# Moving modulation groups to VectorE and reordering the first norm of a fused two-block diffusion transformer

## The chip, the cores and the metric

One core of one Trainium2 chip runs the whole program in one launch. The metric is the device time of one execution in microseconds, as the median of several runs. Next to it stands one profiled execution, whose trace is read here.

## The reference, cut to what matters

Two small transformers run one after the other on 256 tokens `x` and 256 context tokens `ctx`, width 1024, in fp32. The first has two layers (latent attention and a Hyena convolution, then a feed-forward network), the second a gated-delta-rule layer and a gated-linear-attention (GLA) layer, each with its feed-forward network. Each layer takes six modulation vectors of 1024 from a conditioning vector:

```
mod_x = split(silu(c)     @ ada_w + ada_b, 6)     # 1024 x 6144, for x
mod_c = split(silu(c_ctx) @ ada_w + ada_b, 6)     # the same weights, for ctx
h  = rms_norm(x, g) * (1 + mod_x[1]) + mod_x[0]   # ahead of the mixer
x  = x + mod_x[2] * mixer(h)
h  = rms_norm(x, g2) * (1 + mod_x[4]) + mod_x[3]  # ahead of the network
x  = x + mod_x[5] * network(h)
```

The context stream needs chunks 0 and 1 in every layer and chunks 2 to 5 only where its output is used later, which is in the first layer of each transformer.

## The kernel before

**Layout.** Activations lie with features on the 128 partitions: `xs` is [128, 8, 512], x in columns 0 to 255 and ctx in 256 to 511. Every product is made of three fp32r products: a weight tile is split into a high part (`wh`, a cast on ScalarE, L315) and a low part (`wl`, a subtraction on VectorE, L316), activations likewise (L302, L303), and `mm3` (L324 to L326) adds high x high, high x low and low x high. One projection onto 128 features is 24 matmuls. Weights come as 512 KB transfers from SyncE's queue into three buffers.

**Modulation.** There are four matrices of 1024 x 6144: `mods[0]`, `mods[1]` for the first transformer, `mods2[0]`, `mods2[1]` for the second. `modulation` (L375) makes a list of steps, each a load and a computation. In the TensorE form (`steps`, L381) a chunk of 1024 outputs takes eight k tiles, four matmuls of 256 columns each (L402), side by side in strips of 32 columns with both conditioning vectors as the stationary operand; then a copy on ScalarE (L407), two small matmuls (L413) that bring the result into columns, and the bias (L414). In the row form (`rstep`, L434) a group of 128 outputs lies on the partitions with its 1024 weights in a row; one VectorE instruction (L437) multiplies by the conditioning vector `self.cb`, which was spread over the partitions and put through Silu (L588 to L591), and sums along the row. It serves one vector. Before, `mods[1]` and `mods2[1]` use rows for chunks 2 to 5 (32 groups, three in a step) and TensorE for chunks 0 and 1; `mods[0]` and `mods2[0]` use TensorE throughout.

**Where the steps run.** `run` (L1776) puts the steps into a queue, `self.bg`. `background(n)` takes n of them, and `load_ahead` keeps up to two loads (four at the start) ahead of the computation, in buffers of three 512 KB tiles. `quota` says how many steps a stage may take. In a feed-forward network `slot()` is called after each projection and takes a step every `every` slots. There are 56 slots in a network over both streams. Before, the first layer takes the 16 + 12 steps of `mods[0]`, its network the 17 of `mods[1]` and 18 of `mods2[0]` every 1.5 slots, and the deltanet layer's network the 17 of `mods2[1]` every 3.

**The order of the instructions.** The framework's planner orders each engine's instructions: among those that it takes to be ready by its own estimates, the one that is written first comes first. So an instruction that is ready can come ahead of work that is written before it but is not ready. `tc.issue_after` forbids that for a block on one engine. The order is fixed when the program is built; on the chip each engine works through its own.

**The norm.** `stat` adds up squares, `stat_end` takes the mean over features by a matmul with ones (L472) and the root by eleven small VectorE instructions (L457 to L464), `bcast` (L484) spreads the root over the partitions, `norm_one` (L517) makes x * r (L529, or with the factor L527), applies the factor and shift on ScalarE (L537, L540, L541) and makes high and low parts (L538, L542). In layer 0 the factors `gs` (L447, L448) come from chunk 1 of `mods[0]`, whose 16 small steps are the first thing that the program loads.

**Ends of stages.** `first_layer` computes `ys = [self.stat_end(...)]` (L1095) and then, in the return behind it, the same again for layer 0; in layer 1 it returns `S`, and the network (`mlp`, L605) takes the root behind its first projection. In the GLA mixer (`gla`), four heads run in a loop: `values` and `gate` are projections (L1618 to L1620, L1631), `prepare` makes exponentials and products on ScalarE and VectorE, `finish` the scores (L1704), the output (L1721 to L1724, into one PSUM buffer) and its norm (L1729), and `readout` transposes it (L478) and multiplies it by the gate (L1739). Behind the loop the output projection starts with six of eight k tiles for two outputs, and then reads head 3 out (`last`).

## Time and profile before

| | us |
|---|---|
| median of three runs | 2589.76 |
| lowest and highest | 2586.95, 2590.99 |
| the profiled execution | 2585.91 |
| its span, first to last instruction | 2584.1 |
| TensorE busy | 2463.6 |
| VectorE busy | 1721.3 |
| ScalarE busy | 1133.8 |
| GpSimd busy | 235.2 |

The stages by the time order: layer 0 to about 303 us, its network to about 705, layer 1 to 874, its network to about 1065, deltanet to about 1815, its network to about 2165, GLA to 2396, its network to the end. A matmul's record shows its latency; matmuls overlap, so their price in a stream is the distance between two starts. A fp32 matmul (L402, L472, L478, L484) shows as two records.

### The profile page before, as it was taken

Reading aid. Unit: us, or ns where it says so; the run is one execution under the profiler, and the core shown is the slowest. Engines: PE = TensorE matmul, PEld = TensorE weight load, DVE = VectorE, ACT = ScalarE, POOL = GpSimd, SP = SyncE. Lnnn points to the kernel's source line nnn. Section 1 sums busy time; section 2 is a strip of 40 time slices with the busy share of each in tenths; the row PEclk is TensorE's granted clock in tenths of the full one; section 3 lists DMA queues with packets and bytes.
Section 4 is the critical chain, followed back from the end, with each engine's and each line's share of the span. In section 5 each row is a group of like instructions: output and inputs, shape, how many; then the busy total and the mean of one; then the engine's idle time right before and its main releaser. Section 6 shows DMA issues by size and latency. Waiting matters only on the chain.

```text
span 2584.1 us, 39685 instructions
## 1 busy us (share of the span) xinstructions
PE 2463.6 (95%) x15196; PEld 2082.7 (81%) x15196; DVE 1721.3 (67%) x3659; ACT 1133.8 (44%) x2157; POOL 235.2 (9%) x217
## 2 busy tenths in 40 slices
PE   7999999999999899998999999987999999899999
PEld 4766788777886899977778777876878888788999
DVE  5555558333567677898877877878458446777766
ACT  3345423222355455673545444544322334654544
POOL 0000000000000000111233323200000000220000
PEclk8999999999999999999999999999999999999999
DMA  7334468565241456322122212211567332222665
GB/s 273 110 133 150 155 216 323 199 228 174 83 134 63 140 178 206 122 66 56 31 66 66 56 42 68 67 44 50 180 215 256 98 98 82 77 82 72 188 182 156
DMA packets 147359, 335.08 MB, mean 130 GB/s; under 512 B 57134, under 2 KB 68512, under 8 KB 147168
## 3 DMA queue, kind: packets, MB, share of 16 engines
q1 hardware_dynamic: 146912, 332.46, 40.5%
q8 instruction: 120, 1.97, 0.3%
q14 instruction: 71, 0.58, 0.1%
q0 software_dynamic: 256, 0.07, 0.0%
HBM read 328.81 MB, written 3.67 MB: 129 GB/s over the span
## 4 chain that ended last, share of the span: by engine, by line
PE 77%; DVE 10%; issue 5%; ACT 3%; DMA 3%; POOL 1%; SPq 0%; DVEq 0%; ACTq 0%; POOLq 0%
PE pmm L324 19%; PE pmm L326 18%; PE pmm L325 18%; PE pmd L402 2%; DVE wl L316 1%; DMA wm<-wmod 1%; PE ps L1035 1%; ACT wh L315 1%; PE pmm L359 1%; PE pa L1395 1%; PE pa L1371 1%; PE pmm L358 1%; PE pmm L360 1%; PE pa L1413 1%; PE pa L1366 1%
## 5 line engine op out<-in xcount | busy, mean ns | idle before, releaser
L315 ACT CAST wh<-wr 128x1024 fp32r<-128x1024 f32 (+1 forms) x421 | 425.8, 1015 | 687.0 <-PE pmm L325 481.4
L324 PE MATMUL pmm<-h,wh 128*128 128x512 f32 (+2 forms) x1800 | 626.4, 348 | 8.0 <-ACT E L860 1.9
L316 DVE TENSOR_TENSOR wl<-wr,wh 128x1024 fp32r<-128x1024 f32 (+1 forms) x381 | 448.6, 1179 | 275.9 <-ACT wh L315 269.2
L326 PE MATMUL pmm<-h,wl 128*128 128x512 f32 (+2 forms) x1800 | 622.0, 346 | 9.7 <-DVE wl L316 9.7
L325 PE MATMUL pmm<-h,wh 128*128 128x512 f32 (+2 forms) x1800 | 619.1, 344 | 0.0
L326 PE MATMUL pmm<-r,wl 128*128 128x256 f32 (+1 forms) x1280 | 435.0, 341 | 2.6 <-DVE wl L316 2.5
L324 PE MATMUL pmm<-r,wh 128*128 128x256 f32 (+1 forms) x1280 | 435.4, 341 | 1.9 <-DVE q L1020 1.4
L325 PE MATMUL pmm<-r,wh 128*128 128x256 f32 (+1 forms) x1280 | 433.8, 339 | 0.0
L324 PEld LDWEIGHTS pmm<-h,wh 128*128 128x128 f32 x1800 | 342.2, 190 | 56.8 <-issue 6.7
L326 PEld LDWEIGHTS pmm<-h,wl 128*128 128x128 f32 x1800 | 342.5, 190 | 54.2 <-DVE wl L316 11.7
L325 PEld LDWEIGHTS pmm<-h,wh 128*128 128x128 f32 x1800 | 342.5, 190 | 39.5 <-issue 0.8
L324 PEld LDWEIGHTS pmm<-r,wh 128*128 128x128 f32 x1280 | 241.3, 189 | 33.8 <-issue 7.6
L326 PEld LDWEIGHTS pmm<-r,wl 128*128 128x128 f32 x1280 | 241.6, 189 | 28.9 <-DVE wl L316 4.7
L325 PEld LDWEIGHTS pmm<-r,wh 128*128 128x128 f32 x1280 | 241.8, 189 | 23.2 <-issue 1.7
L689 DVE SCALAR_TENSOR_TENSOR xs<-pmm,modb,xs 128x256 f32<-128x256 f32 x232 | 106.6, 478 | 101.6 <-PE pmm L326 101.5
L542 POOL TENSOR_TENSOR h<-n,h 128x256 fp32r<-128x256 f32 x28 | 21.4, 764 | 1218.9 <-ACT h L541 1218.5
L689 DVE SCALAR_TENSOR_TENSOR xs<-pmm,moda,xs 128x256 f32<-128x256 f32 x120 | 54.4, 480 | 110.8 <-PE pmm L326 110.6
L302 ACT CAST r<-h 128x256 fp32r<-128x256 f32 (+1 forms) x128 | 65.7, 514 | 123.6 <-DVE h L640 67.6
L316 POOL TENSOR_TENSOR wl<-wr,wh 128x1024 fp32r<-128x1024 f32 x40 | 96.2, 2406 | 146.8 <-ACT wh L315 112.9
L303 DVE TENSOR_TENSOR r<-h,r 128x256 fp32r<-128x256 f32 (+1 forms) x128 | 71.0, 556 | 32.7 <-ACT r L302 29.8
L437 DVE SCALAR_TENSOR_TENSOR wm<-wm,cb 128x1024 f32<-128x1024 f32 x64 | 76.4, 1220 | 4.2 <-DMA wm<-amodr 2.4
L1397 ACT COPY e<-pa 128x256 f32<-128x256 f32 x64 | 23.8, 372 | 122.5 <-PE pa L1395 121.8
(501 smaller groups left out, 3889.5 us busy)
## 6 DMA issues: line engine op xcount, KB each, us to landing
wr<-w SPq DMA_DIRECT2D x128, 512.0 KB
wr<-f SPq DMA_DIRECT2D x128, 512.0 KB
wr<-dwin SPq DMA_DIRECT2D x49, 512.0 KB
wm<-amod SPq DMA_DIRECT2D x16, 1536.0 KB
wm<-wmod SPq DMA_DIRECT2D x12, 1536.0 KB
wm<-wmodr SPq DMA_DIRECT2D x10, 1536.0 KB
wm<-amodr SPq DMA_DIRECT2D x10, 1536.0 KB
wr<-win SPq DMA_DIRECT2D x28, 512.0 KB
```

The lines of the kernel that those rows point to most:

```text
L302: self.nc.scalar.copy(hi, src)
L303: self.nc.vector.tensor_tensor(lo, src, hi.bitcast(F32), ALU.subtract)
L315: self.nc.scalar.copy(hi, raw)
L316: (self.nc.gpsimd if self.pool_lo else self.nc.vector).tensor_tensor(lo, raw, hi.bitcast(F32), ALU.subtract)
L324: mm(ps, wh[:, k, :], rh[:, n0:n1], start=k == 0, stop=False)
L325: mm(ps, wh[:, k, :], rl[:, n0:n1], start=False, stop=False)
L326: self.mark = mm(ps, wl[:, k, :], rh[:, n0:n1], start=False, stop=k == last)
L358: mm(ps[:, c0:c1], wh[:, k, :], rh[:, c0:c1], start=k == 0, stop=False)
L359: mm(ps[:, c0:c1], wh[:, k, :], rl[:, c0:c1], start=False, stop=False)
L402: self.last = nc.tensor.matmul(ps[32 * c : 32 * c + 32, :256], cs[:, k + i, :], raw[:, i, 256 * c : 256 * c + 256], start=k + i == 0, stop ...
L437: nc.vector.scalar_tensor_tensor(raw[:, i], raw[:, i], 1.0, self.cb, ALU.mult, ALU.mult, accum_out=m[:, i : i + 1])
L689: self.nc.vector.scalar_tensor_tensor(x, ps, mod[:, 8 * gch + m, v : v + 1], x, ALU.mult, ALU.add)
```

## The change

Four things, in the order of the diff:

1. `_rows` gives all 48 groups. With rows, `mods[1]` and `mods2[1]` are made of rows entirely: eight steps of two groups for chunks 0 and 1, with two passes a group (one for each conditioning vector; the product of the second goes into the unused third tile of the buffer), then eleven steps of three groups as before, 19 steps in all and none on TensorE. `mods2[0]` has chunks 2 to 5 on TensorE (12 steps) and 0 and 1 in rows (8 steps). `cb` holds two vectors, 1 MB, and is loaded again with `cb2` ahead of the first step of `mods2[0]`. Quotas and spacing follow: 39 steps every 1.4 slots in layer 0's network, 19 every 2.8 in the deltanet layer's.
2. In layer 0, sums, root and the eight products x * r of the x stream (`norm_pre`) are placed behind the tenth of the 16 steps; `norm_rest` applies the factors later, for odd tiles with a tensor_scalar on VectorE beside ScalarE's.
3. `first_layer` no longer computes `ys` ahead of its return.
4. In the GLA loop, gate 3 comes behind `finish` of head 3, and `readout` of head 2 behind it; `ot` has two buffers.

```diff
         def rstep(j, n, raw):
-            m = mod[:, 16 + j : 16 + j + n, 0]
             for i in range(n):
-                nc.vector.scalar_tensor_tensor(raw[:, i], raw[:, i], 1.0, self.cb, ALU.mult, ALU.mult, accum_out=m[:, i : i + 1])
-            nc.vector.tensor_tensor(m, m, self.small(bname)[:, 16 + j : 16 + j + n], ALU.add)
-
-        rs = [(lambda j=j, n=min(3, 32 - j): rload(j, n), lambda raw, j=j, n=min(3, 32 - j): rstep(j, n, raw)) for j in range(0, 32, 3)]
-        return mod, [s for cc in range(2) for s in steps(cc)] + rs
+
+                for v in (1, 0) if j < 16 else (0,):
+                    nc.vector.scalar_tensor_tensor(raw[:, i if v == 0 else self.wide - 1], raw[:, i], 1.0, self.cb[:, v], ALU.mult, ALU.mult,
+                                                   accum_out=mod[:, j + i, v : v + 1])
+            m = mod[:, j : j + n, :] if j < 16 else mod[:, j : j + n, 0:1]
+            nc.vector.tensor_tensor(m, m, self.small(bname)[:, j : j + n].unsqueeze(2).to_broadcast([P, n, m.shape[2]]), ALU.add)
+
+        js = [(j, 2) for j in range(0, 16, 2)] + ([(j, min(3, 48 - j)) for j in range(16, 48, 3)] if one else [])
+        rs = [(lambda j=j, n=n: rload(j, n), lambda raw, j=j, n=n: rstep(j, n, raw)) for j, n in js]
+        if one:
+            return mod, rs
+        rest = [s for cc in range(2, 6) for s in steps(cc)]
+
+        load, comp = rest[0]
+        rest[0] = load, lambda raw: (self.rows_c("cb2"), comp(raw))[1]
+        return mod, rest + rs
+
+    def rows_c(self, name):
+        self.cb = self.t("cb", 2048).rearrange("p (v n) -> p v n", v=2)
+        self.nc.sync.dma_start(self.cb, self.a[name])
+        self.nc.scalar.activation(self.cb, self.cb, AF.Silu)
...
+    def norm_pre(self, xs, sv, y, tag):
+        rs = self.bcast(y, 2)
+        ts = [self.t(tag, 256) for _ in range(8)]
+        for k, t in enumerate(ts):
+            self.nc.vector.tensor_tensor(t, xs[:, k, sv[0] : sv[1]], rs, ALU.mult)
+        return ts
+
+    def norm_rest(self, out, ts, sv, gs, mod, shch):
...
+            if j % 2:
+                nc.scalar.activation(hi, t, AF.Identity, bias=sh, scale=g)
+                nc.vector.tensor_scalar(t, t, g, sh, ALU.mult, ALU.add)
+            else:
+                nc.scalar.activation(t, t, AF.Identity, bias=sh, scale=g)
+                nc.scalar.copy(hi, t)
+            nc.vector.tensor_tensor(lo, t, hi.bitcast(F32), ALU.subtract)
...
-            self.pools(st, dict(n=(8, 256), h=3, acc=(4, 256), sq=(4, 256), rs=(1, 258), cb=(1, 1024)), dict(a=2, md=1, mm=5), 12 if one else 18, "a", quota)
+            self.pools(st, dict(n=(8, 256), h=3, acc=(4, 256), sq=(4, 256), rs=(1, 258), cb=(1, 2048)), dict(a=2, md=1, mm=5), 12 if one else 18, "a", quota)
...
-        ys = [self.stat_end(S, k) for k in "xc"[:NS]]
         return [self.stat_end(S, k) for k in "xc"] if both else (h, S)
...
-        for hd in range(4):
-            if hd < 3:
-                vn = values(hd + 1)
-                c1 = next(cg)
-            if ot is not None:
+        for hd in range(3):
+            vn = values(hd + 1)
+            c1 = next(cg)
+            if hd:
                 with self.tc.issue_after(self.mark.ins):
                     og += readout(hd - 1, ot, zo)
-            if hd < 3:
+
+            if hd < 2:
                 zn = gate(hd + 1)
-                nxt = prepare(hd + 1, *c1, vn)
+            nxt = prepare(hd + 1, *c1, vn)
             ot, zo = finish(hd, vt, *cur), zs
-            if hd < 3:
-                cur, vt, zs = nxt, vn, zn
+            cur, vt, zs = nxt, vn, zn
+        o3 = finish(3, vt, *cur)
+        zs = gate(3)
+        with self.tc.issue_after(self.mark.ins):
+            og += readout(2, ot, zo)
...
-                        self.background(8)
+                        self.background(4)
 
                         with self.tc.issue_after(self.last.ins):
                             y = self.stat_end(S, "a", 4)
-                        ys = [y[:, :2], y[:, 2:]]
+                            ys = [y[:, :2], y[:, 2:]]
+                            pre = self.norm_pre(xs, both[0], ys[0], "E")
+                        self.background(4)
...
-                    self.ffn(xs, "g2_0", "w1_0", "w2_0", mods[0][0], "2_0", both, ys, None, 35, 1.5, S, None, before, lambda sv: f["then"](sv), cb="cb")
+                    self.ffn(xs, "g2_0", "w1_0", "w2_0", mods[0][0], "2_0", both, ys, None, 39, 1.4, S, None, before, lambda sv: f["then"](sv), cb="cb")
...
-        self.ffn(xs, "fg_0", "f1_0", "f2_0", mods2[0][0], "4", both, None, h, 17, 3, S, None, before, lambda sv: f["then"](sv), [both[1], both[0]], "cb2")
+        self.ffn(xs, "fg_0", "f1_0", "f2_0", mods2[0][0], "4", both, None, h, 19, 2.8, S, None, before, lambda sv: f["then"](sv), [both[1], both[0]], "cb2")
```

## Rows read from the trace of the kernel before

**Rows 1.** Page, part 1: busy us of each engine, share of the span, instructions.

```profile
PE 2463.6 (95%) x15196; PEld 2082.7 (81%) x15196; DVE 1721.3 (67%) x3659; ACT 1133.8 (44%) x2157; POOL 235.2 (9%) x217
```

**Rows 2.** Stretches: length, busy us of each engine (instructions), clock, DMA share, GB/s.

```profile
320.00:340.00 20.00, 20.00 (x176) 19.70 (x178) 2.48 (x6) 4.70 (x12) 2.63 (x4) 1.00 0.01 1
339.00:440.00 101.00, 99.42 (x516) 78.97 (x516) 81.67 (x139) 32.87 (x46) 0.31 (x1) 1.00 0.84 309
440.00:640.00 200.00, 200.00 (x1155) 152.18 (x1155) 73.75 (x106) 51.84 (x68) 0.00 (x0) 1.00 0.61 210
1926.00:1990.00 64.00, 64.00 (x285) 53.02 (x285) 59.36 (x108) 19.30 (x24) 0.00 (x0) 1.00 0.86 305
```

**Rows 3.** Groups by line: count, busy us, mean ns of one, idle before.

```profile
L402 PE MATMUL pmd<-wm,cvs 128*32 128x256 f32 x896 | 59.4, 390 | 1.7 <-DMA wm<-wmod 1.7
L540 ACT ACTIVATE n<-n,modb,gs 128x256 f32<-128x256 f32 x16 | 9.6, 600 | 14.6 <-DVE n L529 14.6
```

**Rows 4.** Order of time, TensorE, around one modulation step: start us, us, instruction.

```profile
475.94 0.39 PE L325 MATMUL pmm<-r,wh 128*128 128x512 f32 x1
476.17 0.39 PE L326 MATMUL pmm<-r,wl 128*128 128x512 f32 x1
476.49 1.50 PE L402 MATMUL pmd<-wm,cvs 128*32 128x256 f32 x24
...
478.25 0.39 PE L325 MATMUL pmm<-r,wh 128*128 128x512 f32 x1
```

**Rows 5.** Order of time, VectorE, one row step of mods[1].

```profile
366.82 1.22 DVE L437 SCALAR_TENSOR_TENSOR wm<-wm,cb 128x1024 f32<-128x1024 f32 x1
...
367.97 1.22 DVE L437 SCALAR_TENSOR_TENSOR wm<-wm,cb 128x1024 f32<-128x1024 f32 x1
...
369.11 1.22 DVE L316 TENSOR_TENSOR wl<-wr,wh 128x1024 fp32r<-128x1024 f32 x1
```

**Rows 6.** Order of time, TensorE and VectorE, before layer 0's first projection.

```profile
40.84 1.87 PE L472 MATMUL pt<-ones,H 128*128 128x1 f32 x8
...
45.15 1.65 PE L484 MATMUL pt<-k_id,rsy 128*128 128x128 f32 x6 [0.58 <-DVE rsy L464]
...
47.98 0.17 DVE L448 TENSOR_TENSOR gs<-gs,g 128x16 f32<-128x16 f32 x1
...
52.45 0.58 PE L359 MATMUL pmm<-h,wh 128*128 128x256 f32 x1 [1.15 <-DVE h L542]
```

**Rows 7.** Order of time, TensorE and VectorE, into the first feed-forward network.

```profile
303.21 0.50 PE L472 MATMUL pt<-ones,sq 128*128 128x1 f32 x4
...
305.04 1.50 PE L472 MATMUL pt<-ones,sq 128*128 128x1 f32 x12 [0.87 <-DVE sq L503]
...
310.59 0.42 DVE L529 TENSOR_TENSOR n<-xs,pa 128x256 f32<-128x256 f32 x1 [0.72 <-PE pa L484]
...
312.75 2.79 PE L402 MATMUL pmd<-wm,cvs 128*32 128x256 f32 x24
```

**Rows 8.** Order of time, TensorE, into the networks behind layer 1 and GLA.

```profile
877.81 0.98 PE L472 MATMUL pt<-ones,xs 128*128 128x1 f32 x4 [4.14 <-DVE xs L503]
...
884.18 0.50 PE L472 MATMUL pa<-ones,xs 128*128 128x1 f32 x4
...
2397.31 0.39 PE L324 MATMUL pmm<-h,wh 128*128 128x258 f32 x1 [1.60 <-DVE xs L689]
...
2400.32 0.50 PE L472 MATMUL pa<-ones,xs 128*128 128x1 f32 x4
```

**Rows 9.** Order of time, TensorE, the waits at the GLA mixer's end.

```profile
2359.53 0.33 PE L478 MATMUL pgt<-k_id,ot 128*128 128x128 f32 x1 [1.22 <-DVE ot L1729]
...
2368.47 1.20 PE L478 MATMUL pgt<-k_id,ot 128*128 128x128 f32 x4 [2.72 <-DVE ot L1729]
...
2370.69 0.58 PE L324 MATMUL pmm<-h,wh 128*128 128x256 f32 x1 [1.01 <-ACT h L302]
```

**Rows 10.** Order of time, ScalarE, the Silu of cb.

```profile
315.35 1.06 ACT L591 ACTIVATE cb<-cb 128x1024 f32<-128x1024 f32 x1
```

More of the change, by code (lines that the diff above doesn't have):

```diff
@@ L424, in modulation @@
             return mod, [s for cc in range(6) for s in steps(cc)]
-        nc.gpsimd.memset(mod[:, 16:, 1], 0.0)
+        rows, one = rows
+        if one:
+            nc.gpsimd.memset(mod[:, 16:, 1], 0.0)
         def rload(j, n):
@@ L507, in stat_end, with norm_mod @@
         return self.rsqrt(a, [P, nb], f"n{key}")
[L511 removed]
+    def norm_mod(self, xs, streams, gs, mod, shch, ys, tag, r=None, pool=False, pre=None):
         out = [self.halves(256 * len(streams), r) for _ in range(8)]
         for sv in streams:
[L514 to L515 removed]
+            if pre:
+                self.norm_rest(out, pre, sv, gs, mod, shch)
+                pre = None
+            else:
+                self.norm_one(out, xs, sv, gs, mod, shch, ys[sv[2]], tag, pool)
+        return out
+    def norm_pre(self, xs, sv, y, tag):
[5 more added lines that the diff above has]
+    def norm_rest(self, out, ts, sv, gs, mod, shch):
+        nc = self.nc
+        c0, c1, v = sv
+        for j, t in enumerate(ts):
+            hi, lo = (o[:, c0:c1] for o in out[j])
+            sh, g = mod[:, 8 * shch + j, v : v + 1], gs[:, j, v : v + 1]
+            if j % 2:
+                nc.scalar.activation(hi, t, AF.Identity, bias=sh, scale=g)
+                nc.vector.tensor_scalar(t, t, g, sh, ALU.mult, ALU.add)
+            else:
+                nc.scalar.activation(t, t, AF.Identity, bias=sh, scale=g)
+                nc.scalar.copy(hi, t)
+            nc.vector.tensor_tensor(lo, t, hi.bitcast(F32), ALU.subtract)
     def norm_one(self, out, xs, sv, gs, mod, shch, y, tag, pool=False):
@@ L588, in ffn @@
             if cb:
-                self.cb = self.t("cb", 1024)
-                self.nc.sync.dma_start(self.cb, self.a[cb])
-                self.nc.scalar.activation(self.cb, self.cb, AF.Silu)
+                self.rows_c(cb)
             self.background(1 if every < 2 else 0)
@@ L1801, in run @@
                         next(filt)
-                        mods = [self.modulation(f"wmod_{j}", f"bmod_{j}", "cv", f"a{j}", 3, 0 if j else 2, "wmodr_1" if j else None) for j in range(2)]
+                        mods = [self.modulation(f"wmod_{j}", f"bmod_{j}", "cv", f"a{j}", 3, 0 if j else 2, ("wmodr_1", True) if j else None) for j in range(2)]
                         self.bg = mods[0][1]
@@ L1836, in early @@
                             self.early = False
-                            mods2.extend(self.modulation(f"amod_{j}", f"abmod_{j}", "cv2", f"b{j}", rows="amodr_1" if j else None) for j in range(2))
+                            mods2.extend(self.modulation(f"amod_{j}", f"abmod_{j}", "cv2", f"b{j}", rows=(f"amodr_{j}", j == 1)) for j in range(2))
                             self.bg = self.bg + mods[1][1] + mods2[0][1] + mods2[1][1]
                             self.quota = 12
-                            return ws, ys
+                            return ws, ys, pre
                         f = dict(h=None, ws=None)
@@ L1931, in run @@
             h = 256
-            sb = dict(n=(6, h), low=1, k=4, q=(4, h), z=(4, h), kE=(2, h), kt=(2, h), S=(4, h), qe=(4, h), Ao=(1, h), part=2, A=(2, P), ot=1)
+            sb = dict(n=(6, h), low=1, k=4, q=(4, h), z=(4, h), kE=(2, h), kt=(2, h), S=(4, h), qe=(4, h), Ao=(1, h), part=2, A=(2, P), ot=2)
             self.pools(st, sb, dict(gt=2, ad=2, po=1, mm=3), 4, "gt")
```

20 lines of the change are left out of this document (9 added, 11 removed).

## The prediction

> **What bounds the kernel now.** I read the page's first part, then the table of stretches, then the instructions in order of time at the five places that the change touches. The page says that TensorE is busy for 95% of the span and VectorE for 67% [rows 1]; so an instruction taken off TensorE counts in full where TensorE has no gap, and one laid on VectorE counts only where VectorE has none. The stretches show where that is. In the first layer's feed-forward network TensorE is busy for all of 440 to 640 us, and VectorE there for 73.75 of 200 us, 37%, which is its load without row steps; while the row steps of `mods[1]` run (339 to 440) VectorE stands at 81.67 of 101 us, and TensorE loses 1.6 us of 101 [rows 2]. In the deltanet's feed-forward network, 1926 to 1990, row steps bring VectorE to 59.36 of 64 us, and TensorE loses nothing [rows 2]. The time order shows four places where TensorE does wait: before the first projection of layer 0, before each of the first two feed-forward networks, and at the end of the GLA mixer.
>
> **Part 1: six chunks of modulation leave TensorE.** Chunks 0 and 1 of `mods[1]`, `mods2[0]` and `mods2[1]` go, 2 x 3. A chunk is 32 matmuls, shown as 64 records: the lines view has 896 records in 59.4 us, so 64 x 66.3 ns = 4.24 us [rows 3]. In place the price is a little higher, since the stream around it breaks: from L326 at 476.17 to the second matmul of the next run at 478.25 are 2.08 us, where two matmuls of that run take 2 x 0.23 = 0.46 us (its pitch, 475.94 to 476.17); a 24-record step thus costs 1.62 us [rows 4], and a chunk (24 + 24 + 16 records) 64/24 x 1.62 = 4.3 us. Beside it stand the two small matmuls of `columns` and the break at them, some 0.3 us (an estimate: another group of four one-shot records takes 0.50 us at 884.18 [rows 8], partly beside its neighbours). I take 4.6 us: 6 x 4.6 = 27.6 us. Bounds: 6 x 4.24 = 25.4 and 6 x 4.9 = 29.4. One step of these ran while TensorE had nothing else, the x24 at 312.75 (2.79 us there [rows 7], where the step of [rows 4] takes 1.50), but the first projection stood behind it, so it counts too.
>
> **What VectorE gets for it.** 16 groups x 2 vectors x 3 = 96 scalar_tensor_tensor passes. One lasts 1.22 us, but the next starts 1.15 us after it (366.82, 367.97, and the next instruction at 369.11) [rows 5]: 96 x 1.15 = 110 us of VectorE, plus 24 bias additions of about 0.15 us. A new two-group step holds VectorE for 4 x 1.15 + 0.15 = 4.75 us. Its due time in the first network is 1.4 slots; a slot is 24 matmuls x 0.231 us = 5.55 us [rows 4], so 7.8 us, of which 63% (by the 37% of 440 to 640) is free: 4.9 us. It fits with almost nothing to spare. Three reasons make me book little loss: VectorE does only 2.48 of 20 us between 320 and 340 [rows 2], where TensorE works on already prepared weights and where three or four of the eight steps of `mods[1]` find room; the stretch at 1926 shows that VectorE at 93% costs TensorE nothing; and in the second network the steps are due every 2.8 slots. Eight steps of `mods2[0]`, late in the first network, have no such room. I book 3 us of TensorE waits, bounds 0 and 17 (working under the rivals). Bytes are the same 512 KB a group either way, so the queue of SyncE carries no more than before; only `cb` grows from 0.5 to 1 MB and is read once more in the first network. That read and its Silu wait for the last row step of `mods[1]`, with the weight loads behind the read on SyncE's queue (three buffers are already under way then). The Silu of 1024 elements takes 1.06 us [rows 10], so 2048 take about 2.1; behind it on ScalarE wait the weight casts, four weights ahead of their matmuls. Cost 0, up to 5 us if the data come later than planned.
>
> VectorE thus runs passes back to back at 1.15 us [rows 5]. [...]
>
> **Part 2: layer 0's first norm.** Now the token mean (1.87 us at 40.84) and the spread of the root (1.65 us at 45.15) stand on TensorE between the last modulation steps and their `columns`; the factor `gs` starts at 47.98, and steady matmuls begin at 52.45, waiting for VectorE [rows 6]. In the new order the mean, the root, its spread and eight products x*r come behind step 10 of 16, where the engines wait for weights. The last columns then come about 1.4 us earlier (the spread no longer ahead of them) and perhaps 0.5 more for the mean. After `gs` come a ScalarE operation (0.60 us each, 9.6 us for 16 [rows 3]), a copy, and a subtraction of 0.42 (as at 310.59 [rows 7]): about 1.5 us, where now 52.45 - 48.15 = 4.3 us pass. Sum 1.4 + 2.8 = 4.2; VectorE still has two weight splits to do there and the weights may land late, so I take 3.5, bounds 0.5 and 5.5. Cover for the eight products: the wait for the last six loads. If it were gone they would stand where they stand now.
>
> **Part 3: the unused root is no longer computed (`ys = ...`, L1095).** In layer 0 four token means are queued where two are needed. The second, 0.87 us of waiting for the last square of the context stream, stands ahead of the one that is used, and the first product of the norm starts at 310.59, 7.4 us after the mean at 303.21 [rows 7]. Alone, the first mean is there at 303.8, its root (11 dependent VectorE operations, 0.2 us apart) at 306.5, the spread 1 us later. So 307.8: 2.8 us, bounds 1.5 and 3.5. Late next is the norm's own chain. In layer 1 the mean is the first thing on TensorE after the projection: it waits 4.14 us for the last square, and the next network's first product runs behind it; from the end of the projection (877.81 - 4.14 = 873.67) to the mean that is used (884.18, behind that first product) are 10.5 us. The GLA mixer ends in the same code without an unused root, and there the same distance is 2400.32 - (2397.31 - 1.60) = 4.6 us [rows 8]. The difference, 5.9 us, is what I take, bounds 3 and 6.5.
>
> **Part 4: the GLA mixer's last head.** TensorE waits 1.22, 2.72 and 1.01 us for head 2's and head 3's outputs [rows 9], 4.95 us together. The new order puts gate 3 (two projections, 48 matmuls of 256 columns, 5.7 us) behind the last head's scores, which fills these. What gate 3 covered before, the preparation of head 3, must then be covered by head 2's scores. I take 4, bounds -2 (a loss) and 7.
>
> **Sum.** 27.6 - 3 + 3.5 + 2.8 + 5.9 + 4 = 40.8 us. The profiled execution took 2585.91 us with a span of 2584.1, and the median of the three runs is 2589.76, 3.9 us above it. The pieces come from the profiled one; I subtract them from the median: 2589.8 - 40.8 = 2549 us.
>
> **The rivals.** (a) *Order changes do nothing*: the start waits for its loads whatever the norm does, and VectorE sets the end of the GLA mixer. For it: [rows 6] show waits, not their reserve. Against it: the waits named end on VectorE and ScalarE. Parts 2 and 4 fall away: 2549 + 7.5 = 2556.5. (b) *VectorE becomes the bound in the first network*. Suppose it can't be used beyond the 81% of 339 to 440. The 19 row steps of `mods[1]` hold 64 x 1.15 + 19 x 0.15 = 76 us, and 26.6 slots need 26.6 x 0.37 x 5.55 = 55 us: 131 / 0.81 = 162 us where TensorE wants 148, 14 us lost; eight steps of `mods2[0]` hold 38 us beside 23: 61 / 0.81 = 75 where TensorE wants 62, 13 lost. The free time from 320 to 340 [rows 2] takes about 10 us off the first, which leaves 17: 2549 + 17 - 3 = 2563; with all 27 it is 2573. Against it: 93% without loss at 1926 [rows 2]. (c) *The other side*: each two-group step holds VectorE for 4.75 us in one piece, and a weight split or residual that comes due behind it makes TensorE wait. It decides from (40.8 + 3) / 24 = 1.8 us of waiting per step; at 3 us per step, 72 us: 2549 - 3 + 72 = 2618, slower. Against it: three-group steps of 3.6 us already run with waits of 1.6 us in all [rows 2]. That all 24 do so at once is unlikely.
>
> **How the numbers follow.** My forecast 0.58, (a) 0.20, (b) 0.15 (one time in three so strong, with (a), that the result lies within 0.2%, about 5 us, of the old time, which is what a measurement of this kernel can tell from no change), (c) 0.07. So faster 0.88, same 0.05, slower 0.07. The low end adds the upper bounds in part: 40.8 + 2 + 3 + 2 + 2 + 3 = 52.8 and since not all come at once I put 2538. The high end takes (b) in full with a weak part 4: 2576. (c) and the rest of (b) stay outside.
>
> **What would show it.** Right: 384 fewer records at L402 (six chunks x 64), and no TensorE gap over 1 us in 440 to 700; VectorE over 90% to about 460 and again at the end of the first network; steady matmuls of the first projection near 49 us; one token mean ahead of the norm at about 300 us, none ahead of the first product of layer 1's network; no 2.72 us wait at L478. Wrong: waits of L326 for L316 in the first network (b, c), or a first projection that starts when it did (a).

## The result, and the profile after

The changed kernel takes 2554.27 us (median of four runs, 2552.22 to 2557.6) against 2588.36 for the kernel before: ratio 0.987, interval 0.9853 to 0.9887. That is 34.1 us less, where 40.8 were forecast. The profiled executions have spans of 2584.1 and 2550.2 us, 33.9 apart, so the pieces below come from these two.

Page, part 1, and then stretches, as in [rows 1, 2] (length, busy us of PE, PEld, DVE, ACT and POOL, clock, DMA share, GB/s; the last two are the eight row steps of `mods2[0]`, and the deltanet's network, in a window 28 us earlier than that of [rows 2]):

```profile
PE 2431.0 (95%) x14776; PEld 2066.8 (81%) x14776; DVE 1827.2 (72%) x3834; ACT 1135.8 (45%) x2152; POOL 238.2 (9%) x217
```

```profile
320.00:340.00 20.00, 19.34 (x131) 17.28 (x129) 19.12 (x34) 9.75 (x16) 1.11 (x1) 1.00 0.53 184
340.00:360.00 20.00, 14.81 (x57) 11.85 (x58) 19.94 (x34) 5.05 (x7) 0.00 (x0) 0.91 0.55 201
339.00:440.00 101.00, 94.46 (x404) 76.39 (x403) 96.71 (x170) 27.17 (x35) 0.00 (x0) 0.98 0.78 286
440.00:640.00 200.00, 200.00 (x1067) 156.68 (x1066) 116.73 (x188) 57.52 (x73) 0.00 (x0) 1.00 0.64 226
567.00:629.00 62.00, 62.00 (x287) 50.66 (x286) 58.54 (x104) 16.30 (x20) 0.00 (x0) 1.00 0.60 205
1898.00:1962.00 64.00, 63.36 (x279) 52.13 (x279) 56.78 (x101) 19.56 (x25) 0.00 (x0) 1.00 0.82 288
```

Groups by line: the chunks that are left on TensorE, the row passes, and the matmul that reads a weight's low part (L325; the last line is the same group, L326, in the kernel before):

```profile
L401 PE MATMUL pmd<-wm,cvs 128*32 128x256 f32 x512 | 33.2, 384 | 0.2 <-DMA wm<-wmod 0.2
L440 DVE SCALAR_TENSOR_TENSOR wm<-wm,cb 128x1024 f32<-128x1024 f32 x160 | 192.7, 1227 | 28.5 <-DMA wm<-amodr 14.1 <-ACT cb L458 10.4 <-DMA wm<-wmodr 3.7
L325 PE MATMUL pmm<-h,wl 128*128 128x512 f32 (+2 forms) x1800 | 623.7, 347 | 18.1 <-DVE wl L315 18.1
L326 PE MATMUL pmm<-h,wl 128*128 128x512 f32 (+2 forms) x1800 | 622.0, 346 | 9.7 <-DVE wl L316 9.7
```

The six chunks are gone from TensorE: 512 records where [rows 3] have 896, 384 fewer, and 32.6 us less busy time. VectorE has 96 passes more (160 for 64) and 106 us more. But between 339 and 440 us TensorE is now busy for 94.46 of 101 us where it was for 99.42 [rows 2], and the wait of L325 for the low part of a weight, 9.7 us in the kernel before, is 18.1. Most of that stands at one place (5.06 us; five smaller waits in this network make 2.0 more). In the order of time, ScalarE, VectorE and TensorE (start, us, instruction, in brackets the wait and what ended it):

```profile
333.25 1.06 ACT L314 CAST wh<-wr 128x1024 fp32r<-128x1024 f32 x1
...
335.47 1.22 DVE L440 SCALAR_TENSOR_TENSOR wm<-wm,cb 128x1024 f32<-128x1024 f32 x1
...
338.42 1.22 DVE L440 SCALAR_TENSOR_TENSOR wm<-wm,cb 128x1024 f32<-128x1024 f32 x1
...
340.77 1.22 DVE L440 SCALAR_TENSOR_TENSOR wm<-wm,cb 128x1024 f32<-128x1024 f32 x1
...
342.51 1.22 DVE L440 SCALAR_TENSOR_TENSOR wm<-wm,cb 128x1024 f32<-128x1024 f32 x1
...
343.66 1.22 DVE L315 TENSOR_TENSOR wl<-wr,wh 128x1024 fp32r<-128x1024 f32 x1
...
344.93 0.80 PE L325 MATMUL pmm<-h,wl 128*128 128x512 f32 x1 [5.06 <-DVE wl L315]
```

The weight has its high part at 334.31, and TensorE multiplies by it from 338.35 on. Its low part, L315, stands behind four row passes and seven other instructions in VectorE's order and starts at 343.66, more than 9 us later. VectorE has no gap there, and TensorE waits 5.06 us. The stretch behind it costs again, since TensorE comes back at half its clock (0.50, 1.2 GHz):

```profile
338.00:344.00 6.00, 1.87 (x9) 1.22 (x7) 6.00 (x11) 2.32 (x4) 0.00 (x0) 1.00 0.00 0
345.00:348.00 3.00, 3.00 (x7) 2.41 (x8) 3.00 (x4) 0.00 (x0) 0.00 (x0) 0.50 0.81 330
```

The start, the first network's norm, layer 1's transition and the GLA mixer's end, to be read beside [rows 6 to 9]:

```profile
34.80 1.87 PE L489 MATMUL pt<-ones,H 128*128 128x1 f32 x8
49.45 0.80 PE L357 MATMUL pmm<-h,wh 128*128 128x256 f32 x2 [3.12 <-ACT h L557]
50.74 0.58 PE L358 MATMUL pmm<-h,wh 128*128 128x256 f32 x1 [0.49 <-DVE h L558]
...
301.66 0.61 PE L489 MATMUL pt<-ones,sq 128*128 128x1 f32 x4 [0.87 <-DVE sq L520]
305.07 0.42 DVE L572 TENSOR_TENSOR n<-xs,pa 128x256 f32<-128x256 f32 x1 [0.63 <-PE pa L501]
306.87 1.01 PE L357 MATMUL pmm<-h,wh 128*128 128x256 f32 x3
...
860.30 0.41 PE L323 MATMUL pmm<-h,wh 128*128 128x258 f32 x1 [0.58 <-DVE xs L730]
863.57 0.50 PE L489 MATMUL pa<-ones,xs 128*128 128x1 f32 x4
871.36 0.42 ACT L518 ACTIVATE acc<-xs 128x256 f32<-128x256 f32 x1 [3.27 <-DMA xs<-ctx]
878.57 0.39 PE L323 MATMUL pmm<-h,wh 128*128 128x258 f32 x1 [2.42 <-DVE h L676]
...
2337.24 0.50 PE L323 MATMUL pmm<-h,wh 128*128 128x256 f32 x2 [1.01 <-ACT h L301]
```

The token mean stands at 34.80 instead of 40.84; the first product of the norm at 305.07 instead of 310.59; no mean stands ahead of layer 1's network, where 4.14 us were waited, and from the end of the projection (860.30 - 0.58) to the mean are 3.85 us instead of 10.5; the 2.72 us wait of the last GLA head is gone.

Laid over each other by token means that both have, the traces give the stages in the table, in us. Its borders are: the first mean behind layer 0's mixer (303.21 in the old kernel, [rows 7]), the context's mean at the end of the first network (700.6), x's mean at the end of layer 1's mixer (884.18, [rows 8]), the means ahead of the deltanet (1069.1), at its end (1794.2), at the end of its network (2167.9) and of the GLA mixer (2400.3), and the end of the span. The other rows are the runs of the next section.

| | layer 0 | first network | layer 1 | its network | deltanet | its network | GLA | last network | span |
|---|---|---|---|---|---|---|---|---|---|
| before | 303.2 | 397.4 | 183.6 | 184.9 | 725.1 | 373.7 | 232.5 | 183.8 | 2584.1 |
| after | 299.8 | 383.6 | 180.2 | 185.8 | 723.4 | 367.5 | 226.0 | 183.9 | 2550.2 |
| after_again | 300.4 | 384.1 | 180.4 | 184.7 | 724.5 | 365.6 | 224.6 | 183.9 | 2548.3 |
| undo_root | 300.4 | 386.8 | 184.3 | 185.2 | 723.2 | 370.0 | 223.8 | 184.1 | 2557.7 |
| undo_gla | 301.1 | 383.6 | 179.7 | 186.8 | 723.1 | 367.0 | 227.8 | 184.1 | 2553.2 |
| undo_norm | 303.9 | 385.9 | 180.3 | 186.1 | 724.3 | 367.4 | 226.3 | 183.9 | 2558.0 |
| undo_mod | 300.4 | 392.8 | 177.7 | 187.1 | 726.7 | 374.3 | 226.2 | 183.8 | 2569.0 |
| one_pass | 301.0 | 374.4 | 181.3 | 189.3 | 724.3 | 371.0 | 225.7 | 183.9 | 2550.8 |
| three_first | 302.7 | 377.8 | 180.1 | 190.8 | 725.1 | 367.3 | 226.1 | 183.9 | 2553.9 |
| interleave | 302.0 | 377.1 | 180.5 | 188.1 | 724.7 | 367.5 | 223.7 | 183.9 | 2547.6 |
| late_squares | 302.7 | 383.6 | 180.9 | 185.8 | 723.2 | 371.5 | 224.4 | 184.1 | 2556.3 |
| mixed_late | 299.7 | 375.2 | 180.3 | 187.1 | 724.2 | 367.4 | 227.4 | 183.9 | 2545.2 |
| own_queue | 301.2 | 399.2 | 179.5 | 188.2 | 723.6 | 380.6 | 224.3 | 184.3 | 2580.9 |

So the 33.9 us come from: layer 0 3.4, the first network 13.8, layer 1 with its network 2.5, the deltanet's mixer, in which nothing was changed, 1.6, its network 6.2, GLA 6.5; the last network takes 0.1 back.

### The profile page after: what moved, and what is told of

Its sections match the earlier page's. It is cut to its first block, busy times and chain, and to the rows that moved or that the text cites. A ratio compares the mean times of both kernels' runs of the same rounds, so it can differ in the third digit from the quotient of the medians.

```text
span 2550.2 us, 39023 instructions
## 1 busy us (share of the span) xinstructions
PE 2431.0 (95%) x14776; PEld 2066.8 (81%) x14776; DVE 1827.2 (72%) x3834; ACT 1135.8 (45%) x2152; POOL 238.2 (9%) x217
## 4 chain that ended last, share of the span: by engine, by line
PE 72%; DVE 14%; issue 5%; ACT 4%; DMA 4%; POOL 1%; SPq 0%; DVEq 0%; ACTq 0%; POOLq 0%
PE pmm L323 17%; PE pmm L325 17%; PE pmm L324 17%; DVE wm L440 2%; DVE wl L315 2%; ACT wh L314 1%; PE ps L1076 1%; PE pmd L401 1%; PE pa L1435 1%; PE pa L1453 1%; PE pa L1411 1%; PE pa L1406 1%; PE pv L1114 1%; DMA wm<-wmodr 1%; PE pa L1399 1%
## 5 line engine op out<-in xcount | busy, mean ns | idle before, releaser
L325 PE MATMUL pmm<-h,wl 128*128 128x512 f32 (+2 forms) x1800 | 623.7, 347 | 18.1 <-DVE wl L315 18.1
L323 PE MATMUL pmm<-h,wh 128*128 128x512 f32 (+2 forms) x1800 | 625.9, 348 | 10.5 <-DVE h L676 2.4
L315 DVE TENSOR_TENSOR wl<-wr,wh 128x1024 fp32r<-128x1024 f32 (+1 forms) x381 | 448.7, 1180 | 205.2 <-ACT wh L314 197.9
L325 PE MATMUL pmm<-r,wl 128*128 128x256 f32 (+1 forms) x1280 | 434.7, 340 | 2.5 <-DVE wl L315 2.4
L325 PEld LDWEIGHTS pmm<-h,wl 128*128 128x128 f32 x1800 | 343.4, 191 | 64.8 <-DVE wl L315 23.2
L325 PEld LDWEIGHTS pmm<-r,wl 128*128 128x128 f32 x1280 | 241.6, 189 | 28.3 <-DVE wl L315 3.9
L440 DVE SCALAR_TENSOR_TENSOR wm<-wm,cb 128x1024 f32<-128x1024 f32 x160 | 192.7, 1227 | 28.5 <-DMA wm<-amodr 14.1
L315 POOL TENSOR_TENSOR wl<-wr,wh 128x1024 fp32r<-128x1024 f32 x40 | 96.1, 2402 | 146.8 <-ACT wh L314 113.0
```

Source lines behind the costliest of these rows:

```text
L315: (self.nc.gpsimd if self.pool_lo else self.nc.vector).tensor_tensor(lo, raw, hi.bitcast(F32), ALU.subtract)
L323: mm(ps, wh[:, k, :], rh[:, n0:n1], start=k == 0, stop=False)
L325: self.mark = mm(ps, wl[:, k, :], rh[:, n0:n1], start=False, stop=k == last)
L440: nc.vector.scalar_tensor_tensor(raw[:, i if v == 0 else self.wide - 1], raw[:, i], 1.0, self.cb[:, v], ALU.mult, ALU.mult, accum_out=mod[ ...
```

## The experiments

Two questions: what each part is worth alone, and what takes back some 8 us in the first network. Each ratio is to the kernel before, measured again beside the run. Theories for the second: T1, VectorE's time and the order in which its work is planned; T2, SyncE's queue, on which weight loads stand behind row loads that wait for a buffer. For T2 speaks that the DMA engines move nothing from 338 to 344 us (share 0.00 above); against it, that the weight whose low part is late had landed before its cast at 333.25.

**undo_root**, part 3 undone.

```diff
         self.dump(f"mix{l}", xs)
+        ys = [self.stat_end(S, k) for k in "xc"[:NS]]
```

> The changed kernel with the unused root put back (part 3 undone alone). By the forecast 2.8 + 5.9 = 8.7 us come back: 2554.3 + 8.7 = 2563.0. By the two traces laid over each other: the spread of the root ends 5.9 us earlier relative to the old kernel ahead of layer 0's network, 3.3 of which were gained before it, so 2.6; at the start of layer 1's network 6.2 us, of which a wait for the network's first hidden tile (2.42 us against 1.09) gives 1.3 back, so 4.9; together 7.5: 2561.8. Rival, the waits behind it absorb it: 2554 to 2556. In the trace: a token mean ahead of the first product of layer 1's network again, with a wait of about 4 us.

Measured 2560.01 us, ratio 0.9894 (0.9879 to 0.9908), some 6 us back in the ratio (0.0024 of 2588) and 7.5 in the span. The first network is 3.0 us longer (average of the two profiles of the changed kernel), layer 1 with its network 3.5 to 4.4. The wait is back:

```profile
865.41 0.99 PE L489 MATMUL pt<-ones,xs 128*128 128x1 f32 x4 [4.05 <-DVE xs L520]
```

At the places themselves the cost shows more sharply than in the stages. From the mean behind layer 0 to the norm's first product are 7.38 us in the kernel before and 7.39 here, against 4.8 to 5.4 in the eleven profiles without the unused root. From the end of layer 1's projection to the mean that is used are 10.5 and 10.1 us, against 3.85 and 5.34 in the two profiles of the changed kernel. So the unused root cost time at both places, about what was forecast; what the stages show less than that in layer 1 is taken up under the reasons below.

**undo_gla**, part 4 undone (the loop over four heads and one buffer for `ot` as in the kernel before).

> The changed kernel with the old order of the GLA mixer's heads (part 4 undone alone). By the forecast 4 us come back: 2558.3. By the traces: 6.3 us at the last head, of which 1.5 us are lost again in a stretch of lower granted clock at the start of the last network: 2559 to 2560.6. Rival, VectorE sets the end of the mixer whatever the order: 2554 to 2555. In the trace: the 2.72 us wait ahead of the transposes of the last head is back.

Measured 2557.55 us, ratio 0.9888 (0.987 to 0.9906). The three waits of [rows 9] are back to the hundredth (1.22, 2.72, 1.01), yet the GLA mixer takes 227.8 us, 1.8 to 3.2 more than in the two profiles of the changed kernel, and not 232.5 as in the kernel before, whose code this is. What differs is the clock. The GLA mixer as one stretch: before, undo_gla, after, after_again:

```profile
2167.90:2400.30 232.40, 207.25 (x1419) 189.03 (x1420) 171.91 (x376) 127.08 (x211) 35.99 (x65) 0.95 0.27 80
...
2141.40:2369.20 227.80, 202.48 (x1420) 184.56 (x1421) 171.89 (x376) 126.92 (x211) 36.53 (x65) 0.98 0.28 82
...
2140.30:2366.30 226.00, 204.65 (x1421) 186.56 (x1421) 171.56 (x376) 126.82 (x211) 36.38 (x65) 0.97 0.27 84
...
2139.30:2363.90 224.60, 203.23 (x1421) 184.75 (x1420) 171.79 (x377) 126.91 (x211) 37.68 (x65) 0.98 0.27 83
```

The mean granted clock was 0.95 in the kernel before and 0.98 here, and TensorE was busy for 4.8 us longer with the same instructions (207.25 and 202.48). The time in which TensorE stands idle, length less busy time, separates the two: 25.15 and 25.32 us with the old order, 21.35 and 21.37 with the new. So of the 6.5 us that the two first profiles show for GLA, 3.8 are idle time that part 4 took away, and 2.6 are busy time at another clock; in undo_gla the better clock hides part of the loss.

**undo_norm**, part 2 undone (sums and root behind the eight last steps, no `norm_pre`).

> The changed kernel with the first layer's norm where it was (part 2 undone alone). By the forecast 3.5 us come back: 2557.8; by the traces 3.1, since every instruction of layer 0's mixer behind the first projection starts 3.13 us earlier than in the kernel before: 2557.4. Rival, the loads set the start whatever the norm does: 2554. In the trace: the last of the first projection's matmuls 3 us later, everything behind it with the same distances.

Measured 2560.06 us, ratio 0.9898 (0.9883 to 0.9912). Layer 0 takes 303.9 us, 3.5 to 4.1 more than in the two profiles of the changed kernel; but the eleven profiles with the new start reach that border between 299.7 and 302.7, on average at 301.0, and the two with the old one at 303.5. So part 2 is worth about 2.5 us there (the ratio gives 4 us against after_again and 7 against the changed kernel's first four runs). The other 4 of the 7.8 us in the span lie in stages that part 2 doesn't touch: the first network, whose code is the same, took 385.9 us. Layer 0 as one stretch, before and after, shows what kind of time it is:

```profile
0.00:303.20 303.20, 285.83 (x1594) 205.63 (x1595) 162.63 (x357) 122.55 (x238) 5.33 (x16) 0.96 0.48 159
...
0.00:299.80 299.80, 282.81 (x1594) 204.35 (x1595) 163.43 (x361) 124.22 (x240) 5.60 (x17) 0.97 0.48 161
```

TensorE's idle time is the same (17.4 and 17.0 us; 16.5 to 18.1 in all thirteen profiles). It is busy for less time with the same instructions, at a mean granted clock of 0.96 in the two profiles with the old start and 0.97 to 0.98 in the eleven with the new one.

**undo_mod**, part 1 undone (the kernel before with parts 2 to 4).

> The kernel before with parts 2, 3 and 4, but its own modulation (six chunks on TensorE, part 1 undone alone). By the forecast 27.6 - 3 = 24.6 us come back: 2578.9. By the traces the modulation brought 13.9 - 2.6 = 11.3 us in the first network, where row steps made TensorE wait, and 6.7 us in the deltanet's network: 18.0 us, 2572.3. Rival, rows cost as much as they save in the first network, and only the deltanet's network gains: 2561 to 2563. In the trace: no wait of 5 us for a weight's low part near 340 us.

Measured 2575.23 us, ratio 0.9951 (0.9936 to 0.9965): 21 us back in the ratio, 18.8 in the span. The first network takes 392.8 us, 9.2 more than after, the deltanet's 374.3, 6.8 more. TensorE has no gap at 340, and VectorE is half idle there:

```profile
320.00:340.00 20.00, 20.00 (x175) 18.14 (x174) 5.89 (x9) 6.97 (x12) 0.00 (x0) 1.00 0.19 61
340.00:360.00 20.00, 20.00 (x125) 15.05 (x124) 10.01 (x16) 6.59 (x10) 0.00 (x0) 1.00 0.91 346
```

**one_pass**, half the passes for the first eight row steps, the same loads.

```diff
...
-                for v in (1, 0) if j < 16 else (0,):
+                for v in (1, 0) if j < 16 and rows != "wmodr_1" else (0,):
...
```

> The changed kernel with one pass in place of two for the 16 groups of chunks 0 and 1 of mods[1] (the context stream's half is left out); loads, their bytes and their queue stay. T1, VectorE's own time: it is busy for all of 340 to 380 us, and the 5.06 us wait for a weight's low part stands behind row passes; 16 x 1.15 = 18.4 us less of them end the waits of that stretch (5.06, 0.53, 0.26), the lower granted clock after it (about 1.6) and perhaps the late ones (1.2): 2554 - 7 to 9 = 2545 to 2547. T2, SyncE's queue: the weight loads stand behind row loads that wait up to 10.2 us for a buffer, and the DMA engines move nothing from 338 to 344; a buffer comes free after 2.3 us of passes in place of 4.6, so half of that stays: about 2550, with idle DMA and a wait of 2 to 3 us near 340.

The first network takes 374.4 us, 9.2 less than after, and behind the norm the only wait in it over 0.15 us is one of 1.06 us. The stretches show VectorE at 16.68 of 20 us where it was at 19.12:

```profile
320.00:340.00 20.00, 18.94 (x134) 17.47 (x133) 16.68 (x30) 7.28 (x12) 1.10 (x1) 1.00 0.68 252
340.00:360.00 20.00, 20.00 (x90) 16.58 (x89) 19.65 (x32) 9.67 (x14) 0.00 (x0) 1.00 0.73 263
```

T1 holds, as far as this stage goes. It also gives the price of a chunk: 392.8 - 374.4 = 18.4 us for four chunks, 4.6 each (4.9 if the 1.06 us wait is taken off). The whole took 2548.23 us (two runs, 2543.88 and 2552.59), ratio 0.9848 (0.982 to 0.9875), less of a gain than the stage's: layer 1's network and the deltanet's network were each 3.5 us longer than after.

**own_queue**, the row loads issued by GpSimd.

```diff
-            nc.sync.dma_start(raw[:, :n], self.a[rows][j : j + n].rearrange("k p n -> p k n"))
+            nc.gpsimd.dma_start(raw[:, :n], self.a[rows][j : j + n].rearrange("k p n -> p k n"))
```

> The changed kernel with the row loads issued by GpSimd in place of SyncE, everything else as it was: no weight load stands behind a row load. T2, the queue: no idle DMA at 338 to 344, weights land early, the 5 us wait goes: 2547 to 2549. T1, VectorE's time: the passes are as many as before and VectorE stays full from 340 to 380, so TensorE waits about as long, somewhere in that stretch: 2553 to 2556.

Measured 2579.59 us, ratio 0.9968 (0.9956 to 0.9979), slower than after by more than either theory said. No weight load can stand behind a row load now, and the wait is there all the same (TensorE in the order of time):

```profile
346.54 0.80 PE L325 MATMUL pmm<-h,wl 128*128 128x512 f32 x1 [5.44 <-DVE wl L315]
```

The weight's high part was made from 339.26 to 340.31; its low part, L315, starts at 345.26, behind four row passes. T2 falls as the cause of that wait. The new loss has two places in this network. One is a queue again, GpSimd's: its load waits 7.85 us for a buffer that VectorE still works in, six of the norm's subtractions stand behind it, and TensorE waits 5.43 us for them (GpSimd and TensorE in the order of time).

```profile
317.03 0.74 POOL L433 DMA_DIRECT2D wm<-wmodr  x1 [7.85 <-DVE wm L440]
317.79 4.63 POOL L585 TENSOR_TENSOR h<-n,h 128x256 fp32r<-128x256 f32 x6
318.58 0.58 PE L358 MATMUL pmm<-h,wh 128*128 128x256 f32 x1 [5.43 <-POOL h L585]
```

The other is the second read of `cb`. It is issued at 455.77, ScalarE comes to its Silu before the data are there, and the part of the hidden tile that stands behind it on ScalarE keeps TensorE waiting for 6.68 us (ScalarE and TensorE):

```profile
465.85 1.91 ACT L458 ACTIVATE cb<-cb 128x2048 f32<-128x2048 f32 x1 [4.29 <-DMA cb<-cb]
469.75 0.80 PE L323 MATMUL pmm<-r,wh 128*128 128x512 f32 x1 [6.68 <-ACT r L301]
```

In the changed kernel this read is issued at 443.93, the Silu starts at 454.60 without a wait, and TensorE has no gap there. The deltanet's network, where the row loads have the new queue too, took 13.1 us more.

**three_first**, the three-group steps ahead of the two-group ones.

```diff
-            return mod, rs
+            return mod, rs[8:] + rs[:8] if rows == "wmodr_1" else rs
```

> The changed kernel with the order of mods[1]'s row steps turned: the eleven three-group steps (3 passes, 3.6 us) first, then the eight two-group ones (4 passes, 4.75 us). T1, VectorE's time: in the first 60 us of the network each step holds VectorE 1.15 us less, some 8 steps, 9 us, enough to end the 5 us wait: 2547 to 2550, with waits of 1 us or less later. T2, the queue: a step now loads 1.5 MB in place of 1, so the weights behind it come later, not earlier: 2554 to 2558, the wait near 340 as long or longer.

The first network takes 377.8 us, 5.8 less; the longest wait in it behind the norm is 1.66 us, where T2 forecast one as long or longer, and all of them make 2.1 us (7.1 in the changed kernel). VectorE does the same passes and is as full as before, and from 339 us on TensorE loses next to nothing:

```profile
339.00:440.00 101.00, 100.83 (x439) 82.54 (x439) 99.26 (x171) 32.27 (x42) 0.00 (x0) 0.99 0.77 275
360.00:410.00 50.00, 50.00 (x223) 41.40 (x222) 50.00 (x91) 11.54 (x12) 0.00 (x0) 1.00 0.83 306
```

So it is not VectorE's share: at 98% TensorE is busy for 100.83 of 101 us, at 96% in the changed kernel for 94.46. What differs is the order: the second low part of the network stands behind 12 row passes here and behind 16 in the changed kernel. The whole is 2553.04 us, ratio 0.9868 (0.9839 to 0.9897), no better than after, which T1 did not expect: 2 to 3 us are lost in layer 0, whose code is the same, and 5.0 in layer 1's network, where TensorE waits 4.96 us for L676.

**interleave**, ten of the TensorE steps of `mods2[0]` between the row steps.

```diff
...
+                            r, t = mods[1][1], mods2[0][1]
+                            mix = [s for i in range(10) for s in r[2 * i : 2 * i + 2] + t[i : i + 1]]
-                            self.bg = self.bg + mods[1][1] + mods2[0][1] + mods2[1][1]
+                            self.bg = self.bg + mix + t[10:] + mods2[1][1]
```

> The changed kernel with ten of the TensorE steps of mods2[0] set between the row steps of mods[1], two row steps and then one on TensorE, so that VectorE's row work is spread over the network: 96 passes and what is left, 110 + 0.37 x 365 = 245 us of 365. T1: VectorE is under 90% at 340 to 440, the waits of 5.06, 0.53, 0.26, 1.2 us and the lower clock behind them go: 2554 - 8 = 2546, faster than either kernel. T2, the queue: the TensorE steps load 1.5 MB each and hold their buffer until TensorE comes to them, so weights still stand behind them: 2552 to 2556.

The first network takes 377.1 us, 6.5 less, the wait near 340 is 2.06 us. Measured 2549.65 us, ratio 0.9851 (0.9836 to 0.9866), 3.6 us more than T1 said and less than T2 said; the second read of `cb` stands behind the ten steps here. Layer 1's network again is longer (188.1), with a wait of 3.27 us for L676.

**late_squares**. In both reordered runs layer 1's network gave back part of what the first one won (5.0 of 5.8 us, 2.3 of 6.5). L676, the first product of the hidden tiles, stands on VectorE behind sums of squares of the second context, whose load is issued only behind layer 1's mean. The edit moves those squares behind the first hidden tiles.

```diff
-                        nc.vector.tensor_tensor(u, ps, rs, ALU.mult)
-                        nc.scalar.activation(t, u[:, :256], AF.Relu, bias=u[:, 256:257])
+                        m1 = nc.vector.tensor_tensor(u, ps, rs, ALU.mult)
+                        self.hm = m1, nc.scalar.activation(t, u[:, :256], AF.Relu, bias=u[:, 256:257])
...
-                            for k in range(8):
-                                self.stat(S, "c", xs[:, k, 256:])
+                            with self.tc.issue_after(self.hm[0].ins), self.tc.issue_after(self.hm[1].ins):
+                                for k in range(8):
+                                    self.stat(S, "c", xs[:, k, 256:])
```

> The changed kernel with one edit outside the change: in layer 1's network the squares of the second transformer's context tokens come behind the first hidden tiles on VectorE and ScalarE (their load starts only behind layer 1's token mean). Theory, part 3 is partly given back there: in the changed kernel the first product of the hidden tiles (L676) stands on VectorE behind sums of squares (L520) that wait until 871.4 for that load, and TensorE waits 2.42 us for it, where it waited 1.09 before; then the wait falls to 1 us or less and layer 1's network is 1.5 to 3 us shorter: 2551.5 to 2553. Rival, the weights behind the load set the pace of that start: the wait moves to a weight's low part and nothing is gained, 2554.

The wait for L676 falls from 2.42 to 0.53 us, as expected, but layer 1's network takes 185.8 us, the same as after: the context's mean, which stands on TensorE, now waits for the moved squares.

```profile
880.35 0.39 PE L323 MATMUL pmm<-h,wh 128*128 128x258 f32 x1 [0.53 <-DVE h L676]
...
942.49 0.58 PE L489 MATMUL pa<-ones,acc 128*128 128x1 f32 x4 [1.61 <-DVE acc L520]
```

So the order is what makes L676 wait for that load, but this edit only moved the wait. 2551.25 us, ratio 0.9863 (0.9844 to 0.9882), can't be told from after.

**mixed_late**, three-group steps first, interleaved, and the late squares.

> Both corrections: in the first network the three-group steps first, ten TensorE steps of mods2[0] between the row steps, and the squares of the second context late as in the run before. If VectorE's early load and those squares are what the change lost: first network 6 to 9 us shorter, layer 1's network 2 to 4 us shorter than with the mixed order alone: 2554.3 - 8 to 12 = 2542 to 2546, faster than both kernels. Rival, gains in one stage are given back by waits and lower clock further on: 2549 to 2552.

Measured 2543.83 us, ratio 0.9832 (0.9817 to 0.9847), below both kernels: its interval against the kernel before lies under that of the changed kernel. The first network takes 375.2 us, 8.4 less than after, as expected; layer 1's network 187.1, only 1.0 less than in interleave, where 2 to 4 were expected. In the first network VectorE is busy for 75% of the stretch in which it was for 96%, and TensorE for all of it:

```profile
339.00:440.00 101.00, 101.00 (x506) 79.99 (x505) 75.69 (x125) 29.34 (x37) 0.00 (x0) 1.00 0.81 298
```

**after_again**, the changed kernel unedited.

> The changed kernel once more, nothing edited: what differs between two profiled executions of one program. If the places of the lower granted clock are the program's own, every stage has its length of the first profile within 0.3 us. If they differ between executions, stages differ by 1 to 3 us with no edit, and stage differences of that size in the other runs (part 4: 6.4 us by the two profiles, 1.8 us when undone alone) mean nothing by themselves. Time 2554 within 0.2%.

Measured 2555.66 us, ratio 0.9882 (0.9865 to 0.9898). The wait near 340 is there again, 5.07 us. The stages differ by up to 1.9 us (the deltanet's network 367.5 and 365.6) without an edit. So the first alternative is wrong, and a difference of 2 us in one stage of one pair of profiles says nothing.

## Why the prediction was right, and where it was off

The range and the sign were right. The sum was 7 us too high, and nearly all of that lies in one term, what VectorE makes TensorE wait. The pieces below don't add up to the last microsecond, since a stage of one unedited program differs by up to 2 us between two profiles.

- **What a chunk costs on TensorE: right.** 4.6 us forecast, 4.6 to 4.9 by undo_mod against one_pass.
- **What VectorE makes TensorE wait: the mis-sized term.** The passes themselves cost VectorE 106 us where 110 were forecast. For what that makes TensorE wait, 3 us were booked (bounds 0 and 17) on three reasons. Measured: in the first network 9.2 us of the 18.4 stayed away (undo_mod to after), 7.1 of them as waits of L325 for a weight's low part; in the deltanet's 0.5 to 2.4 of 9.2 by the two profiles of the changed kernel. The reason that failed is "VectorE does only 2.48 of 20 us between 320 and 340": the passes did go there (19.12 of 20 us), and still VectorE stayed full to 380. It counted free time, and not the order: a weight's low part that comes due stands behind passes planned ahead of it. That is the mechanism of rival (c), which was given 3 us for each of 24 steps and a chance of 0.07; it came at one step with 5.06 us and a few small ones. Rival (b) had the size nearer but the place wrong: it took 13 us for the eight steps of `mods2[0]`, and these ran from 567 to 629 without a TensorE gap, with VectorE at 94%. The second reason, 93% without loss at 1926, thus held, and three_first shows it more strongly (98%); the third, 2.8 slots in the second network, held but for waits of 0.95, 0.43 and 0.64 us (one of 0.69 in after_again).
- **Queue and `cb`.** "Cost 0" stands for the changed kernel: with the row loads on another queue the wait for the low part stayed (own_queue), and the second read of `cb` leaves no gap. The reserve of "up to 5 us if the data come later than planned" was real: in own_queue they did, and TensorE waited 6.68 us.
- **Part 2**: 3.5 forecast, 2.5 by the averages. Steady matmuls were to begin near 49 and begin at 50.74 (50.4 to 52.7 in the other kernels with the new order, 52.45 and 52.74 with the old). The prediction had weight splits on VectorE as the reserve; what stands ahead of the first high part is also a weight's cast in ScalarE's order (48.06, 1.03 us), and the first matmul waits 3.12 us for that part. Of the 3.4 us between the two first profiles the matmuls' start gives 1.7; the rest goes with the clock, which is back at its upper level in the stretch from 55 to 60 (1.00, in the kernel before 0.71). The prediction had no term for the clock:

```profile
55.00:60.00 5.00, 5.00 (x44) 5.00 (x43) 4.63 (x13) 3.78 (x9) 0.00 (x0) 1.00 0.71 249
```

- **Part 3**: 2.8 forecast for layer 0, 3.0 by the stages, 2.0 to 2.6 at the place. 5.9 for layer 1: at the place the distance fell from 10.5 to 3.85 and 5.34 in the two profiles, by 5.2 to 6.65, but undone alone the part is worth 3.5 to 4.4 in the stages. The first product of the hidden tiles is not what takes the rest back. L676 comes 7.2 us behind the first square of the second context in every profile whose squares stand ahead of it, and that square starts when its load lands, 6.45 to 10.32 us behind the mean; so TensorE's wait is 1.09 us in the kernel before, 2.42 and 1.31 in the two profiles of the changed kernel, and 1.80 in undo_root. What is longer is the stretch ahead of the projection's end, from the end of the first network: 176.3 and 175.1 us, 174.2 in undo_root and 173.1 in the kernel before. But for its last 20 us TensorE's idle time in it is alike in the four (6.4 to 6.8 us) and the mean granted clock is 0.99 in the first two and 1.00 in the others, so here too part of the difference is clock; whether part 3 has a hand in that isn't shown.
- **Part 4**: 4 forecast, 3.8 to 4.0 us of idle time measured. Of the three waits that it named (4.95 us) two went, 3.94 us; the third, 1.01 us at the output projection, stayed. The rest of the 6.5 us in the profiles is clock.
- **Not forecast**: 1.6 us in the deltanet's mixer, where nothing was edited. Over the thirteen profiles, all with the same code there, it takes 723.1 to 726.7 us, so this is within their spread.

Of what was to show it, the count of L401, no TensorE gap over 1 us from 440 to 700, the lone mean at 300, none ahead of layer 1's network and no 2.72 us wait came true. VectorE over 90% did in part: 96% to 440 us, where the row steps ended (not 460), and 94% from 567 to 629. The start near 49 did not come; and the sign of rivals (b) and (c), L325 waiting for L315 in the first network, was there.

## What to carry to other kernels

Neither free time of an engine in a table of stretches nor its share says whether pieces of more than a microsecond fit. VectorE at 96% cost TensorE 6.5 us of 101 with one order of the steps, and at 98% 0.2 us with another. What counts is what comes due while a piece runs, and where the planner has put it in the order; so look at the order of time where the other engine first needs something new. Mixing the new work with steps that stay (75% here) was the fastest kernel, but it was tried together with two other edits. And before a gain at one wait is written down, look for the next thing on the same engine that waits for a load; measure each part alone, and more than once, since two profiles of one program differ by 2 us in a stage.

## What the runs showed of the hardware

**The same waits, and another clock behind them.** The same three waits at the end of GLA (1.22, 2.72, 1.01 us) stand in the kernel before and in undo_gla, whose code is the same there. In 11 us from about the end of the second of them the mean granted clock is 0.55 in the one and 0.84 in the other, and the mixer takes 232.5 us in the one and 227.8 in the other:

```profile
2369.00:2380.00 11.00, 9.07 (x42) 8.08 (x42) 6.20 (x12) 4.46 (x9) 0.00 (x0) 0.55 0.26 76
...
2338.00:2349.00 11.00, 8.53 (x53) 7.63 (x54) 7.37 (x15) 5.62 (x11) 0.00 (x0) 0.84 0.22 58
```

**Row passes can be slower beside GpSimd.** A row pass takes 1.22 us, but 1.76 and 1.75 while GpSimd subtracts in the norm of the first network (the changed kernel, in the order of time):

```profile
311.95 1.22 DVE L440 SCALAR_TENSOR_TENSOR wm<-wm,cb 128x1024 f32<-128x1024 f32 x1 [0.27 <-ACT cb L458]
312.29 5.72 POOL L585 TENSOR_TENSOR h<-n,h 128x256 fp32r<-128x256 f32 x4 [2.25 <-ACT h L584]
...
313.98 1.76 DVE L440 SCALAR_TENSOR_TENSOR wm<-wm,cb 128x1024 f32<-128x1024 f32 x1
...
315.67 1.75 DVE L440 SCALAR_TENSOR_TENSOR wm<-wm,cb 128x1024 f32<-128x1024 f32 x1
```

The pass at 311.95 began ahead of the first of the four subtractions and was not longer; that subtraction took 1.49 us, where the ones before it took 0.75.

The Trainium skill, page "SBUF — State Buffer", section "Who interferes with whom", says that a VectorE instruction with two inputs in SBUF contends with a GpSimd instruction that reads SBUF; the trace agrees, with 1.76 for 1.22 us. No run here takes GpSimd's work away from that place, so that the shared access is the cause is not shown.
